# Two-layer encoder on one core: the feed-forward block in column order, with a pair's products reordered and the down lo parts on VectorE

## The chip, the cores and the metric

One of the cores of a Trainium2 chip runs the whole program. Its engines are TensorE (PE; its weight loads are listed as PEld), VectorE (DVE), ScalarE (ACT), GpSimd (POOL) and SyncE (SP), which issues nearly all transfers. The metric is the device time of one execution in microseconds, median of the runs shown.

## What is computed

```python
for l in range(DEPTH):                     # 2 layers
    x = x + hybrid_mixer(rms_norm(x, norm_mix[l]), ...)            # neighbourhood + grouped-query attention
    x = x + memory_cross_attention(rms_norm(x, norm_mem_q[l]), ...)
    x = x + conv_ffn(rms_norm(x, norm_ffn[l]), w_up[l], conv_w[l], conv_b[l], w_down[l])
return rms_norm(x, norm_final)

def conv_ffn(h, w_up, conv_w, conv_b, w_down):
    u = h @ w_up                                                    # (512, 1024) @ (1024, 5632)
    up = jnp.pad(u, ((0, 0), (1, 1), (0, 0)))
    u = up[:, :-2] * conv_w[0] + up[:, 1:-1] * conv_w[1] + up[:, 2:] * conv_w[2] + conv_b
    gate, val = jnp.split(u, 2, axis=-1)
    return (jax.nn.silu(gate) * val) @ w_down                       # (512, 2816) @ (2816, 1024)
```

There are 512 tokens on a grid of 8 rows and 64 columns, and the width is 1024. The convolution runs over the sequence, in which a token's neighbour is the next column of its row. All is float32.

## The kernel before

Activations are kept transposed: channels on the 128 partitions, the 512 tokens along a row. `xT` holds the 1024 channels in 8 chunks. The tokens stand there in column order: 8 grid rows of one column side by side, then the next column. So the sequence neighbour of a token lies 8 places on, and where a grid row ends, at the row's end of another place.

Every float32 product is made of three reduced-precision ones: an operand is split into a rounded part (`hi`, written by ACT) and the rest (`lo`, written by DVE or POOL as the difference), and `mm3` adds hi x hi, hi x lo and lo x hi in one PSUM bank.

The feed-forward block works through 22 channel pairs (a gate and a value block of 128 channels each). The first `N_PLAIN` pairs are *plain*: 24 products of 512 columns a side (`up_project`), whose sum is multiplied by the norm's factor on the way (`rep`), since the norm is not known when they start. The others are *grouped* pairs (`up`): the product of the two sides is built from seven smaller ones of 256 columns, for which DVE, ACT and POOL form sums of the weight blocks (`combined`: parts "11", "12", "22" and s1 to s4) and once a layer sums of the normed activations (`operands`: "11", "21", "22", t1 to t4). Seven products of 12 matmuls make 84 of 256 columns. A pair's last product is put off behind the first products of the next pair (`left`, `finish_up`).

`up_finish` evicts a pair: ACT multiplies by the middle tap and adds the bias, DVE adds the two neighbour taps, ACT applies SiLU to the gate, DVE multiplies gate and value, ACT and DVE write the product's hi and lo part into `acts`. Before, the block ran in row order: closing rows of the norm, scalings by `rep`, operand building and storing of activations had one side of the access pattern strided (`rows`, `lines`), so that a convolution tap was one shift by one place.

The activations of the first 16 pairs (but 2 and 3) lie in two buffers of the tag `xg`, of which there are two, and which hold the normed input until the last plain pair has read it. With them go *grouped downs* (`down_grouped`): in 16 steps of 24 products of 512 columns the activations of four pairs are multiplied and added to `xT`. `behind(n)` says which of these steps follow pair n. The remaining pairs are multiplied in `down` or `down_last`.

PSUM has 8 banks: 4 with the tag `mm`, 2 each with `sc` and `tr`. Weights come through three `raw` buffers in the order of `weights()`, and a letter there says who writes the lo part ("P" POOL, "D" DVE).

The order of the instructions is not the order of the code. All calls are taped first; then a planner runs through the tape with costs of its own for each instruction, under the plans of `PLANS` (patience, reach, a margin, rounds), and issues the whole program in the best order that it finds. An engine executes its list strictly in order.

## Time and profile before

| | before |
|---|---|
| median of 3 runs | 1319.98 us (1318.95 to 1320.20) |
| profiled execution | 1318.78 us, span 1316.9 us, clock 0.999 |
| PE busy | 1295.7 us (98%), 7557 matmuls |
| DVE busy | 1118.4 us (85%), 1805 instructions |
| ACT busy | 811.6 us (62%) |
| POOL busy | 738.6 us (56%) |
| the first layer's feed-forward block | about 292 to 660 us |
| the second layer's | about 943 to the end |

In the profile an instruction is named by what it writes and reads: `xg<-t,xg` writes an activation's lo part from a temporary `t` and its hi part in `xg`; `lo<-raw,hi` is a weight's lo part; `hi<-t,hi`, `lo<-t,lo` and `r<-raw,r` are lo parts of the weight sums and blocks of a grouped pair; `t<-sc,par,t` and `t<-tr,minus,t` are convolution taps; `mm`, `sc`, `tr` are PSUM tiles. Since every call passes through one helper, all rows have the same line, L400, and rows are told apart by their names. Matmuls overlap their successors, so a row's mean for one is longer than the distance from start to start.

### The profile page before, as it was taken

The page shows a single profiled execution, that of the slowest core. Times are in us where ns is not written, and L with a number is a line of the kernel's source. Part 1 is how long each engine was busy: PE and PEld are TensorE (multiplying, and loading weights), DVE is VectorE, ACT ScalarE, POOL GpSimd, SP SyncE. Part 2 cuts the span into 40 slices and gives each one's busy share as a digit, 9 for nine tenths or more (in the row PEclk, how much of TensorE's full clock was granted, in tenths as well). Part 3 has the DMA queues.
Part 4 walks back from the last instruction along what each step waited for, and adds up shares of the span by engine and source line. Part 5 has one row for each costly group of instructions (what it writes and reads, how often), then busy time and mean ns, then how long its engine had stood idle before and what let it go on. Part 6 is the DMA issues. An engine that isn't in the chain of part 4 may idle for free.

```text
span 1316.9 us, 20628 instructions
## 1 busy us (share of the span) xinstructions
PE 1295.7 (98%) x7557; PEld 1137.1 (86%) x7557; DVE 1118.4 (85%) x1805; ACT 811.6 (62%) x1526; POOL 738.6 (56%) x559
## 2 busy tenths in 40 slices
PE   9999999999999999999999999999999999999998
PEld 8898888887779999999888988888787899999997
DVE  8689896769999999998655898966799999999874
ACT  7777686565655656555537767765646556555552
POOL 4555867626645556544727557774456455554460
PEclk9999999999999999999999999999999999999999
DMA  8742313313222332233355422232132232233331
GB/s 279 235 129 64 97 49 98 95 49 97 80 80 97 110 115 97 97 97 112 122 159 176 129 74 72 80 97 81 48 112 64 83 111 96 98 114 113 100 106 65
DMA packets 42901, 137.48 MB, mean 104 GB/s; under 512 B 5040, under 2 KB 8496, under 8 KB 42800
## 3 DMA queue, kind: packets, MB, share of 16 engines
q1 hardware_dynamic: 42224, 135.51, 32.4%
q8 instruction: 60, 0.98, 0.3%
q10 hardware_dynamic: 576, 0.66, 0.1%
q14 instruction: 41, 0.34, 0.1%
HBM read 126.18 MB, written 2.10 MB: 97 GB/s over the span
## 4 chain that ended last, share of the span: by engine, by line
PE 77%; DVE 19%; issue 2%; ACT 1%; DMA 1%; POOL 0%; SPq 0%; DVEq 0%; ACTq 0%
PE mm L400 47%; PE sc L400 15%; PE tr L400 15%; DVE t L400 7%; DVE r L400 3%; DVE xg L400 2%; DVE lo L400 1%; DVE mm L400 1%; DVE xT L400 1%; DVE sc L400 1%; DVE hi L400 1%; DVE tr L400 1%; ACT r L400 1%; DVE s L400 0%; DMA raw<-in_w 0%
## 5 line engine op out<-in xcount | busy, mean ns | idle before, releaser
L400 POOL TENSOR_TENSOR lo<-raw,hi 128x512 fp32r<-128x512 f32 (+2 forms) x196 | 341.9, 1758 | 265.6 <-ACT hi L400 250.7
L400 PE MATMUL mm<-xg,hi 128*128 128x512 f32 (+1 forms) x898 | 282.3, 393 | 5.1 <-ACT xg L400 2.5
L400 ACT CAST hi<-raw 128x512 fp32r<-128x512 f32 (+2 forms) x212 | 160.4, 782 | 71.5 <-PE mm L400 29.3
L400 PEld LDWEIGHTS mm<-xg,hi 128*128 128x128 f32 x898 | 164.2, 188 | 39.5 <-DVE xg L400 6.6
L400 PE MATMUL mm<-r,hi 128*128 128x512 f32 (+1 forms) x608 | 193.1, 388 | 0.4 <-DVE xg L400 0.4
L400 PE MATMUL mm<-xg,lo 128*128 128x512 f32 (+1 forms) x449 | 174.9, 389 | 0.0
L400 POOL TENSOR_TENSOR t<-raw,raw 128x512 f32<-128x512 f32 x64 | 92.7, 1469 | 139.2 <-DMA raw<-in_w 117.4
L400 PE MATMUL sc<-r,r 128*128 128x256 f32 (+1 forms) x760 | 132.9, 309 | 0.0
L400 PEld LDWEIGHTS mm<-r,hi 128*128 128x128 f32 x608 | 112.2, 188 | 22.4 <-DVE xg L400 1.2
L400 PE MATMUL mm<-r,lo 128*128 128x512 f32 (+1 forms) x336 | 123.2, 367 | 0.0
L400 PE MATMUL sc<-r,hi 128*128 128x256 f32 (+1 forms) x800 | 113.2, 288 | 0.7 <-ACT t L400 0.7
L400 PEld LDWEIGHTS sc<-r,r 128*128 128x128 f32 x760 | 106.3, 191 | 5.9
L400 PE MATMUL mm<-hi,xg 128*128 128x512 f32 (+1 forms) x384 | 108.0, 357 | 0.0
L400 POOL TENSOR_SCALAR t<-t,s 128x512 f32<-128x512 f32 (+1 forms) x112 | 66.8, 612 | 73.0 <-DVE s L400 63.4
L400 PE MATMUL tr<-r,lo 128*128 128x256 f32 x768 | 102.9, 283 | 3.8 <-ACT t L400 3.8
L400 PEld LDWEIGHTS sc<-r,hi 128*128 128x128 f32 x800 | 102.7, 192 | 3.2 <-ACT t L400 2.0
L400 DVE TENSOR_TENSOR r<-raw,r 128x512 fp32r<-128x512 f32 x96 | 102.9, 1083 | 2.0 <-ACT r L400 1.8
L400 POOL TENSOR_TENSOR t<-t,raw 128x512 f32<-128x512 f32 x64 | 101.1, 1579 | 4.9
L400 PE MATMUL tr<-r,r 128*128 128x256 f32 x768 | 102.7, 283 | 0.6 <-DVE t L400 0.6
L400 PEld LDWEIGHTS tr<-r,r 128*128 128x128 f32 x768 | 98.7, 191 | 3.8 <-issue 1.4
L400 PEld LDWEIGHTS tr<-r,lo 128*128 128x128 f32 x768 | 96.7, 192 | 4.4 <-ACT t L400 4.4
L400 PEld LDWEIGHTS mm<-xg,lo 128*128 128x128 f32 x449 | 84.4, 188 | 17.3
(158 smaller groups left out, 2845.8 us busy)
## 6 DMA issues: line engine op xcount, KB each, us to landing
raw<-in_w SPq DMA_DIRECT2D x207, 512.0 KB, 3.6
r<-r SPq DMA_DIRECT2D x30, 256.0 KB, 3.5
r<-in_bias SPq DMA_DIRECT2D x16, 384.0 KB, 5.1
raw<-in_w SPq DMA_DIRECT2D x8, 384.0 KB, 3.1
r<-in_memT SPq DMA_DIRECT2D x4, 512.0 KB, 6.5
xT<-in_w SPq DMA_DIRECT2D x7, 256.5 KB, 4.3
r<-in_w SPq DMA_DIRECT2D x9, 128.0 KB, 4.1
t<-in_memT SPq DMA_DIRECT2D x4, 256.0 KB, 5.9
```

What stands on the lines that cost most here:

```text
L400: call(*args, **kwargs)
```

## The change

The feed-forward block stays in column order throughout. The closing rows, the scalings, the operand building and the stores lose their strided views; the convolution's taps shift by 8 places, in two pieces a tap: 504 columns, and 7 more where the neighbour lies in the next grid row. `N_PLAIN` goes from 6 to 7. Plain pairs are evicted in the order in which they are computed, pair j-2 after pair j, with the stores of all seven kept for the end; banks alternate by j % 4. In a grouped pair the product "12" x "21" moves from second to fifth place, while the previous pair's last product still stands behind the second. The grouped downs' steps follow other pairs (two each behind pairs 9 and 12), the activations of pairs 8 to 11 go to other places of the ring (`SLOTS`), the lo parts of their weights are written by DVE, and the planner is given six plans of four rounds in place of three of three.

```diff
-N_PLAIN = 6
+N_PLAIN = 7
...
+SLOTS = {j: j % KC if j < 8 or j > 11 else (2, 3, 0, 1)[j - 8] for j in range(N_GROUPED)}
...
 def behind(n):
-    return [] if n < N_PLAIN else range(0 if n == N_PLAIN else n - BEHIND, min(n - BEHIND + 1, N_GROUPED))
+    at = lambda r: (7, 8, 9, 9, 10, 11, 12, 12)[r] if r < 8 else r + BEHIND
+    return [r for r in range(N_GROUPED) if at(r) == n]
...
-PLANS = [((60.0, 300.0, 300.0, 300.0, 0.0), 300, margin, ASIDE, 3) for margin in (40.0, 80.0, 120.0)]
+PLANS = [((60.0, *[patience] * 3, 0.0), 300, margin, ASIDE, 4) for patience in (60.0, 120.0) for margin in (80.0, 120.0, 160.0)]
...
             hi, lo = self.ops[c]
-            if self.gcol == G_FFN:
-                hi, lo = (v.rearrange("p (r c) -> p c r", r=ROWS) for v in (hi, lo))
-                src = src.rearrange("p (c r) -> p c r", r=ROWS)
...
-                us[side] = get_w(("up", j, side)), ps_mm() if j < 2 else ps_t() if side else ps_s()
+                us[side] = get_w(("up", j, side)), ps_mm() if j % 4 < 2 else ps_t() if side else ps_s()
...
-                    DVE.tensor_mul(lines(pm), lines(pm), rows(ffn.rep))
-                up_finish(j, pms)
+                    DVE.tensor_mul(pm, pm, ffn.rep)
+                return up_finish(j, pms)
+            stores = []
             for j in range(2, N_PLAIN):
...
-                if j < 4:
-                    finish(j)
-            for j in (0, 1, *range(4, N_PLAIN)):
-                finish(j)
+                stores.append(finish(j - 2))
+            for j in range(N_PLAIN - 2, N_PLAIN):
+                stores.append(finish(j))
+            for store in stores:
+                store()
...
-                    DVE.scalar_tensor_tensor(lines(v), rows(xT[k]), par[:, l, G_FFN + k : G_FFN + k + 1], rows(ffn.psum),
+                    DVE.scalar_tensor_tensor(v, xT[k], par[:, l, G_FFN + k : G_FFN + k + 1], ffn.psum,
...
-            product(y, w["12"], "21", True)
-            finish_up()
             product(v, w["s1"], "t1", True)
             ACT.copy(p5, v)
+            finish_up()
             product(x, w["s2"], "t2", False)
             ACT.copy(sums[:, 1], x)
+            product(y, w["12"], "21", False)
             product(v, w["s4"], "22", False)
...
-                DVE.scalar_tensor_tensor(cc[:, 1:], u[:, : S - 1], w[0], cc[:, 1:], op0=ALU.mult, op1=ALU.add)
-                DVE.scalar_tensor_tensor(cc[:, : S - 1], u[:, 1:], w[2], cc[:, : S - 1], op0=ALU.mult, op1=ALU.add)
+                for wi, dst, src in (
+                    (w[0], slice(8, S), slice(0, S - 8)),
+                    (w[0], slice(1, 8), slice(S - 8, S - 1)),
+                    (w[2], slice(0, S - 8), slice(8, S)),
+                    (w[2], slice(S - 8, S - 1), slice(1, 8)),
+                ):
+                    DVE.scalar_tensor_tensor(cc[:, dst], u[:, src], wi, cc[:, dst], op0=ALU.mult, op1=ALU.add)
...
-            hi, lo = (rows(v) for v in acts[j])
-            ACT.copy(hi, lines(cs[0]))
-            DVE.tensor_sub(lo, lines(cs[0]), f(hi))
+            def store():
...
+                hi, lo = acts[j]
+                ACT.copy(hi, cs[0])
+                DVE.tensor_sub(lo, cs[0], f(hi))
+
+            return store
...
-        return placed(("down", g, m), "w_down", [*range(4 * g, 4 * g + 4)] * 2, [P * m] * 4 + [P * (m + 4)] * 4, "P")
+        return placed(("down", g, m), "w_down", [*range(4 * g, 4 * g + 4)] * 2, [P * m] * 4 + [P * (m + 4)] * 4, "D")
```

Three places show how instructions move. The first is DVE's list in the first layer's plain pairs. Before (`mm_753`, `mm_766` are the two sides of pair 0, `mm_770`, `mm_783` those of pair 1, `sc_824`, `tr_828` those of pair 3, `hi_846` a weight sum of the first grouped pair):

```order
L400 TENSOR_TENSOR mm_783<-mm_783,rep_760 128x512
L400 SCALAR_TENSOR_TENSOR t_850<-mm_753,par,t_850 128x511
L400 TENSOR_TENSOR r_834<-t_832,r_833 128x512
L400 SCALAR_TENSOR_TENSOR t_851<-mm_766,par,t_851 128x511
L400 SCALAR_TENSOR_TENSOR t_856<-sc_824,par,t_856 128x511
L400 SCALAR_TENSOR_TENSOR t_857<-tr_828,par,t_857 128x511 x2
L400 SCALAR_TENSOR_TENSOR t_856<-sc_824,par,t_856 128x511
L400 SCALAR_TENSOR_TENSOR t_854<-mm_770,par,t_854 128x511
L400 TENSOR_TENSOR hi_846<-t_843,hi_846 128x512
```

Now, right behind the norm's factor (`xT_76,par,tr_761` are the first instructions of the operand building):

```order
L404 TENSOR_TENSOR mm_753<-mm_753,rep_760 128x512
L404 TENSOR_TENSOR mm_766<-mm_766,rep_760 128x512
L404 SCALAR_TENSOR_TENSOR t_771<-xT_76,par,tr_761 128x512
L404 TENSOR_TENSOR mm_770<-mm_770,rep_760 128x512
L404 SCALAR_TENSOR_TENSOR t_772<-xT_78,par,tr_761 128x512
L404 TENSOR_TENSOR r_775<-t_771,r_775 128x256
L404 SCALAR_TENSOR_TENSOR t_792<-xT_76,par,tr_761 128x512
L404 SCALAR_TENSOR_TENSOR t_776<-t_776,t_772 128x256
L404 SCALAR_TENSOR_TENSOR t_798<-mm_753,par,t_798 128x504
L404 SCALAR_TENSOR_TENSOR t_777<-t_776,t_772 128x256
L404 SCALAR_TENSOR_TENSOR t_798<-mm_753,par,t_798 128x7
```

The convolution of pair 0 has moved from behind that of later pairs, among the weight sums of the first grouped pair, to the head of the block.

The second place is DVE's list in a step of the grouped pairs. Before:

```order
L400 TENSOR_TENSOR sc_963<-sc_963,t_965 128x512
L400 TENSOR_TENSOR lo_977<-t_974,lo_977 128x512
L400 TENSOR_TENSOR lo_979<-t_972,lo_979 128x512
L400 TENSOR_TENSOR hi_978<-t_975,hi_978 128x512
L400 SCALAR_TENSOR_TENSOR t_991<-sc_963,par,t_991 128x511 x2
L400 TENSOR_TENSOR r_971<-raw_938,r_971 128x512
L400 TENSOR_TENSOR xg_853<-t_967,xg_852 128x8x64
L400 TENSOR_TENSOR r_993<-raw_962,r_993 128x512
L400 TENSOR_TENSOR xT_76<-xT_76,mm_981 128x512
```

Now:

```order
L404 SCALAR_TENSOR_TENSOR t_1030<-sc_999,par,t_1030 128x504
L404 TENSOR_TENSOR xT_77<-xT_77,mm_1006 128x512
L404 TENSOR_TENSOR xg_867<-t_1003,xg_866 128x512
L404 TENSOR_TENSOR r_1032<-raw_1005,r_1032 128x512
L404 SCALAR_TENSOR_TENSOR t_1030<-sc_999,par,t_1030 128x7
L404 SCALAR_TENSOR_TENSOR t_1030<-sc_999,par,t_1030 128x504
L404 TENSOR_TENSOR xT_79<-xT_79,mm_1007 128x512
L404 SCALAR_TENSOR_TENSOR t_1030<-sc_999,par,t_1030 128x7
L404 TENSOR_TENSOR lo_1023<-raw_998,hi_1022 128x1024
L404 TENSOR_TENSOR r_1033<-raw_1019,r_1033 128x512
```

The two taps of a side have become four instructions in place of two, the store of an activation (`xg_867`) is contiguous, and a down weight's lo part of 1024 columns (`lo_1023`) has come in.

The third place is POOL's list in the same stretch. Before:

```order
L400 TENSOR_TENSOR lo_912<-raw_889,hi_911 128x1024
L400 TENSOR_TENSOR t_925<-raw_890,raw_908 128x512
L400 TENSOR_TENSOR t_924<-raw_890,raw_908 128x512
L400 TENSOR_TENSOR t_926<-t_924,raw_890 128x512
L400 TENSOR_TENSOR t_927<-t_926,raw_908 128x512
L400 TENSOR_TENSOR lo_936<-raw_913,hi_935 128x1024
```

Now:

```order
L404 TENSOR_TENSOR t_1036<-raw_1005,raw_1019 128x512
L404 TENSOR_TENSOR t_1035<-raw_1005,raw_1019 128x512
L404 TENSOR_TENSOR t_1037<-t_1035,raw_1005 128x512
L404 TENSOR_TENSOR t_1038<-t_1037,raw_1019 128x512
L404 TENSOR_TENSOR t_1060<-raw_1025,raw_1043 128x512
```

Only the four weight sums of a pair are left there.

More of the change, by code (lines that the diff above doesn't have):

```diff
@@ L1511, in encoder_kernel @@
         acts = {}
-        rows = lambda v: v.rearrange("p (c r) -> p r c", r=ROWS)
-        lines = lambda v: v.rearrange("p (r c) -> p r c", r=ROWS)
         def up_project(j, side, ks, us):
             if us[side] is None:
-                us[side] = get_w(("up", j, side)), ps_mm() if j < 2 else ps_t() if side else ps_s()
+                us[side] = get_w(("up", j, side)), ps_mm() if j % 4 < 2 else ps_t() if side else ps_s()
             w, pm = us[side]
@@ L1627, in last @@
                 product(x, w["22"], "t4", False)
-                up_finish(j, [gate, val], True)
+                up_finish(j, [gate, val], True)()
             left.append(last)
@@ L1650, in up_finish @@
             DVE.tensor_mul(cs[0], cs[0], cs[1])
-            if j < N_GROUPED and j not in (2, 3):
-                if not ring:
-                    ring.extend(xpool.tile([P, KC, S], F32R, tag="xg", name=nm("xg"), bufs=2) for _ in range(2))
-                acts[j] = [v[:, j % KC] for v in ring]
-            else:
-                acts[j] = rpair()
-            hi, lo = (rows(v) for v in acts[j])
-            ACT.copy(hi, lines(cs[0]))
-            DVE.tensor_sub(lo, lines(cs[0]), f(hi))
+            def store():
+                if j < N_GROUPED and j not in (2, 3):
+                    if not ring:
+                        ring.extend(xpool.tile([P, KC, S], F32R, tag="xg", name=nm("xg"), bufs=2) for _ in range(2))
+                    acts[j] = [v[:, SLOTS[j]] for v in ring]
+                else:
+                    acts[j] = rpair()
+                hi, lo = acts[j]
+                ACT.copy(hi, cs[0])
+                DVE.tensor_sub(lo, cs[0], f(hi))
+            return store
         ring = []
```

## The prediction

> **What bounds the kernel now.** I read the page first, then busy time by stage of the two feed-forward blocks, then TensorE's waits there, then the chain of waits, and last the groups of instructions.
>
> ```profile
> span 1316.9 us, 20628 instructions
> PE 1295.7 (98%) x7557; PEld 1137.1 (86%) x7557; DVE 1118.4 (85%) x1805; ACT 811.6 (62%) x1526; POOL 738.6 (56%) x559
> PE 77%; DVE 19%; issue 2%; ACT 1%; DMA 1%; POOL 0%; SPq 0%; DVEq 0%; ACTq 0%
> ```
>
> TensorE is busy for 98%; whatever the change brings has to come out of some 21 us of idle TensorE. The profiled execution took 1318.78 us, 1.88 us more than its span and 1.20 us below the median of 1319.98. I make the sum against 1318.78 and add 1.2 at the end.
>
> By stage (us, then busy us and count of PE, PEld, DVE, ACT, POOL; clock; DMA):
>
> ```profile
> 292.00:312.00 20.00, 18.48 (x77) 13.41 (x76) 19.48 (x27) 13.00 (x17) 12.26 (x9) 1.00 0.17 56
> 340.00:395.00 55.00, 50.52 (x262) 42.52 (x261) 54.62 (x70) 32.82 (x51) 29.43 (x17) 1.00 0.24 77
> 395.00:487.00 92.00, 91.35 (x633) 85.40 (x632) 91.23 (x103) 53.34 (x89) 52.10 (x31) 1.00 0.31 104
> 487.00:625.00 138.00, 138.00 (x967) 129.72 (x966) 128.10 (x150) 79.39 (x132) 73.81 (x44) 1.00 0.32 103
> 990.00:1046.00 56.00, 51.51 (x267) 43.37 (x266) 55.66 (x70) 33.80 (x53) 29.95 (x17) 1.00 0.24 76
> ```
>
> The first layer's block starts near 292. TensorE idles 1.5 us while the last norm rows close, 4.5 us from 340 to 395 (last plain pairs, first grouped pair), 0.65 us in the next six pairs and nothing after. The second layer repeats it (4.5 us from 990 to 1046). DVE is 99% busy wherever TensorE waits. The chain of waits from 290 to 395 names it, and the timeline shows the waits (start, duration, in brackets the idle time and its releaser):
>
> ```profile
> by line: DVE t L400 34.8%; DVE xg L400 12.8%; DVE r L400 11.6%; issue 8.0%; DVE mm L400 6.3%; DVE sc L400 5.4%; DVE xT L400 5.0%; DVE lo L400 4.9%; DVE tr L400 4.3%; DVE hi L400 2.5%; POOL s L400 2.2%; DVE s L400 1.3%; ACT xg L400 1.2%; ACT
> ...
> 298.74 0.39 PE L400 MATMUL mm<-r,lo 128*128 128x512 f32 x1
> 300.24 0.74 PE L400 MATMUL mm<-xg,hi 128*128 128x512 f32 x2 [1.11 <-DVE xg L400]
> 302.45 0.68 PE L400 MATMUL mm<-xg,hi 128*128 128x512 f32 x2
> 303.20 0.98 PE L400 MATMUL mm<-xg,hi 128*128 128x512 f32 x2
> ...
> 341.71 0.70 PE L400 MATMUL tr<-xg,hi 128*128 128x512 f32 x2 [1.36 <-DVE t L400]
> ...
> 375.56 1.69 PE L400 MATMUL tr<-r,lo 128*128 128x256 f32 x12 [1.53 <-ACT t L400]
> 378.49 1.20 PE L400 MATMUL mm<-xg,hi 128*128 128x512 f32 x4 [1.24 <-ACT xg L400]
> ```
>
> At 341 a plain pair waits for a PSUM bank whose predecessor DVE has not finished; at 375 and 378 the first grouped pair and the first down product wait for activations of pairs 0 and 1, which DVE evicted late. So the start of the block is DVE-bound, the rest TensorE-bound with DVE at its heels.
>
> **The change, part by part.** *TensorE's work.* One more plain pair in each layer: 48 products of 512 columns for 84 of 256. From start to start, in a stretch without waits:
>
> ```profile
> 441.66 1.60 PE L400 MATMUL sc<-r,r 128*128 128x256 f32 x12
> 443.10 1.60 PE L400 MATMUL tr<-r,r 128*128 128x256 f32 x12
> ...
> 452.37 0.61 PE L400 MATMUL mm<-xg,hi 128*128 128x512 f32 x2
> ...
> 453.05 0.61 PE L400 MATMUL mm<-xg,hi 128*128 128x512 f32 x2
> ```
>
> Twelve of 256 take 1.44 us, 0.120 each; three of 512 (two and one) take 0.68, 0.227 each. 48 x 0.227 - 84 x 0.120 = +0.82 us a layer, **+1.7 us**, certain because TensorE has no slack. Reordering a pair's products costs TensorE nothing; it starts with the sums' operands and needs the block "12" last.
>
> *Strided operands go.* DVE and ACT groups (busy us, mean ns):
>
> ```profile
> L400 DVE TENSOR_TENSOR sc<-sc,t 128x512 f32<-128x512 f32 x32 | 22.0, 688 | 1.0 <-PE sc L400 1.0
> L400 DVE SCALAR_TENSOR_TENSOR t<-xT,par,tr 128x512 f32<-128x512 f32 x16 | 18.8, 1206 | 0.0
> L400 DVE TENSOR_TENSOR tr<-tr,rep 128x512 f32<-128x512 f32 x8 | 9.1, 1133 | 0.0
> L400 DVE SCALAR_TENSOR_TENSOR r<-mm,s,r 128x512 fp32r<-128x512 f32 x8 | 5.9, 748 | 8.8 <-ACT r L400 8.8
> L400 DVE SCALAR_TENSOR_TENSOR xg<-sc,par,xg 128x512 fp32r<-128x512 f32 x4 | 4.4, 1152 | 0.0
> L400 DVE SCALAR_TENSOR_TENSOR r<-mm,s,r 128x128 fp32r<-128x128 f32 x8 | 2.8, 344 | 1.0 <-ACT r L400 1.0
> L400 DVE TENSOR_SCALAR s<-s,s 128x1 f32<-128x1 f32 x96 | 17.4, 205 | 0.4
> L400 DVE TENSOR_TENSOR lo<-raw,hi 128x1024 fp32r<-128x1024 f32 x8 | 11.4, 1451 | 0.1
> ...
> L400 ACT CAST hi<-t 128x512 fp32r<-128x512 f32 x64 | 39.6, 619 | 8.0 <-POOL t L400 7.8
> L400 ACT CAST xg<-t 128x512 fp32r<-128x512 f32 x28 | 33.3, 1205 | 23.3 <-DVE t L400 23.3
> ```
>
> Column order makes these contiguous. A scaling by the norm falls from 1.13 to 0.69, the operand building from 1.21 to 0.75, the lo part of a closing row from 1.15 to 0.75, ACT's casts from 1.2 to 0.62. Up to the first grouped pair DVE saves, in a layer, 12 x 0.44 + 8 x 0.46 + 8 x 0.40 = 12 us in a stretch whose chain is DVE; the seventh plain pair gives back about 6 us there (two scalings, four conv passes, a product and a lo part), but TensorE is given 10.9 us more in the same stretch. The convolution now shifts by 8 columns: two pieces of 504 and two of 7 a side in place of two of 511. A 7-wide piece stands nowhere in the trace. Bounds: 0.13 us (several `s<-s,s` of 0.205 run overlapped) and 0.344 (the 128-wide form); the two sizes of `r<-mm,s,r` extrapolate to 0.22. I take 0.18 with some overlap, nearest to the 1-wide row: four a pair, +0.7 us.
>
> [...]
>
> *Closing rows.* The last row's chain is ACT's hi, then DVE's lo: 0.5 + 0.4 = 0.9 us shorter, against the 1.27 us that TensorE loses from 298.74 (1.50 from start to start less 0.227). At 303.20 two products take 0.98 instead of 0.68; that throttling by rows of 1.15 us happens twice and goes too. I take 1.2 us a layer (bounds 0.5 and 2.0): **-2.4 us**.
>
> *Arrival-order eviction.* Pairs 0 and 1 are scaled, convolved and multiplied as soon as their sums stand, pairs 4 and 5 take `mm` banks so that `tr` and `sc` come round less often, and only the stores wait for the last plain pair. The waits 1.36, 1.53 and 1.24 go, each with some 0.16 of overlap around it, and 0.3 at 368: 4.9 us a layer, and I count **-9.8 us**. What is late next is the operand building, which holds one of the two `tr` banks until its last instruction.
>
> *Down lo parts on DVE.* This loads the engine that has no idle time. In the six pairs from 395 to 487:
>
> ```profile
> L400 DVE TENSOR_TENSOR r<-raw,r 128x512 fp32r<-128x512 f32 x18 | 22.9, 1273 | 0.1
> L400 DVE TENSOR_TENSOR hi<-t,hi 128x512 fp32r<-128x512 f32 x12 | 12.8, 1068 | 0.0
> L400 DVE TENSOR_TENSOR lo<-t,lo 128x512 fp32r<-128x512 f32 x12 | 11.7, 1011 | 0.0
> L400 DVE TENSOR_TENSOR xg<-t,xg 128x512 fp32r<-128x512 f32 x7 | 10.3, 1476 | 0.0
> L400 DVE TENSOR_TENSOR t<-t,t 128x512 f32<-128x512 f32 x6 | 7.9, 1322 | 0.1
> ...
> L400 POOL TENSOR_TENSOR lo<-raw,hi 128x1024 fp32r<-128x1024 f32 x7 | 18.5, 2640 | 19.3 <-ACT hi L400 17.4 <-PE mm L400 1.9
> ```
>
> Instructions with both inputs in SBUF take 1.01 to 1.32 us on average where one with a PSUM input takes 0.69: they stand still while POOL works. Surplus over 0.69 (1.13 for the strided xg): 18 x 0.58 + 12 x 0.38 + 12 x 0.32 + 7 x 0.35 + 6 x 0.63 = 25 us, against 52.1 us of POOL busy: 0.48 us of standstill for each us of POOL. So DVE's 15.2 us a pair are 11.1 of its own and 4.1 of standstill. After: 11.1 + 1.2 (a lo part of 1024 without standstill, from 0.69 and its 512 more columns; 1.45 with) - 0.45 (contiguous xg) + 0.7 = 12.5, and POOL's time falls from 8.7 to (52.1 - 18.5) / 6 = 5.6, so standstill to 2.7: **15.2 us of DVE against 15.5 of TensorE** (84 x 0.120 + 24 x 0.227). It fits, barely, and two of the first six pairs now carry two grouped products (5.5 us more for TensorE, 2.6 for DVE). I charge 1.5 us of new waits a layer (bounds 0 and 8), **+3 us**. Behind a late DVE stand the operands of the next pair, `tr` and `sc` banks, and the down lo parts themselves, three raw buffers deep.
>
> [...] Moving 2.4 us off POOL for 1.2 on DVE lowers their sum, but a lo part on DVE can now itself be held; that is the rival below.
>
> The planner draws up the whole program anew, so rows move elsewhere too; TensorE idles so little there that I allow ±1 us and count nothing.
>
> Sum: 1.7 - 2.4 - 9.8 + 3.0 = -7.5; 1318.8 - 7.5 = 1311.3 profiled, **1312.5 us** as a median.
>
> **The rivals.** *A: slower, DVE becomes the bound of the grouped pairs.* Place: DVE's queue between two pairs. If standstill stays at 4.1 us because the additional two-input instruction meets POOL as often, and the 7-wide pieces cost 0.22 in full, a step takes 12.7 + 4.1 = 16.8 us, 1.3 over. Over 14 steps that is 18 us, less 6 for the two double steps and about 4 that two banks of each kind can absorb: 8 to 10 us a layer. 1.7 - 2.4 - 9.8 + 19 = +8.5: **1328 us**. It decides from a step of about 16.3 us on. For it: DVE is at 99% today, and every us put on it is real. Against it: POOL loses a third of its time.
>
> *B: the waits only move.* The store of pairs 0 and 1 still needs the activation buffer, which opens only when the last plain pair has been multiplied; and the `tr` bank of the operand building comes free at about the same point as its next user. If half of the 9.8 us stays and 3 us of new waits come, 1.7 - 2.4 - 4.9 + 6 = 0: **1320 us**. Against it: the work between (convolution, multiplication) is done earlier, and only 0.62 + 0.69 us a pair remain behind the buffer.
>
> *C: better than forecast.* No new waits, all of the closing throttle gone and the 0.65 us in mid-block too: 1.7 - 4 - 11 = -13: **1306.5 us**.
>
> **How the numbers follow.** Forecast 0.57, C 0.13, B 0.17, A 0.13. A difference under 0.2% (2.6 us) can't be told from none. Faster: forecast and C, 0.70, with a little of B, 0.71; same: the rest of B and the weak end of the forecast, 0.16; slower: A, 0.13. The forecast's own range, from its bounds, is 1308 to 1317. The range that holds 8 in 10 takes in most of C and B and the mild part of A: 1306 to 1322.
>
> **What would show it.** Right: the stretch that answers to 340 to 395 has TensorE idle under 1.5 us in place of 4.5, the row at 298 shows under 0.5, DVE's two-input rows with a mean near 0.95, POOL busy lower by some 75 us, DVE busy near 1118 still, at 97% in the grouped pairs. Wrong: TensorE waits from the second grouped pair on, released by DVE hi, lo or r, with two-input means above 1.1 (A), or idle time near 350 and 380 as before under other names (B). A 7-wide row with a mean over 0.3 would break the sum's weakest term.

## The result, and the profile after

The changed kernel takes **1303.78 us** (median; 1303.15 to 1304.09) where the kernel before took 1319.47 beside it (1317.9 to 1320.2): a ratio of 0.9882, 95% interval 0.9865 to 0.9899. The forecast was 1312.5 in a range of 1306 to 1322. The direction was right, the gain was twice the one forecast, and the time fell below the range. The span went from 1316.9 to 1301.1 us.

The page of the changed kernel (span; busy time of each engine; the chain of waits by engine):

```profile
span 1301.1 us, 20672 instructions
PE 1291.9 (99%) x7485; PEld 1135.6 (87%) x7485; DVE 1066.1 (82%) x1999; ACT 777.3 (60%) x1510; POOL 655.8 (50%) x523
PE 94%; POOL 1%; DVE 1%; issue 1%; ACT 1%; DMA 0%; SPq 0%; DVEq 0%; POOLq 0%
```

DVE's share of the chain went from 19% to 1%, TensorE's from 77% to 94%. DVE executes 194 more instructions and is busy for 52 us less. By stage, with the columns of the prediction's table; the rows answer to the block's start, the stretch around the first grouped pair, the first and the later grouped pairs, and the first grouped pair of the second layer:

```profile
292.00:312.00 20.00, 20.00 (x91) 16.59 (x90) 18.62 (x31) 12.39 (x21) 12.66 (x9) 1.00 0.34 100
340.00:395.00 55.00, 55.00 (x290) 47.48 (x290) 55.00 (x91) 32.81 (x54) 28.79 (x18) 1.00 0.30 95
395.00:503.00 108.00, 108.00 (x731) 100.37 (x730) 103.69 (x158) 59.29 (x106) 43.48 (x28) 1.00 0.35 113
503.00:616.00 113.00, 113.00 (x789) 106.12 (x789) 93.66 (x151) 58.66 (x102) 42.08 (x27) 1.00 0.29 91
990.00:1038.00 48.00, 48.00 (x262) 41.81 (x261) 48.00 (x82) 28.82 (x49) 22.17 (x14) 1.00 0.28 88
```

TensorE does not idle in any of them, where it had idled 1.5 us at the start and 4.5 us a layer around the first grouped pair. From 340 to 395 DVE is still busy without a gap, but nothing waits for it any more. The last closing row and the first product that reads the normed input, in the timeline (start, duration):

```profile
301.02 0.39 PE L404 MATMUL mm<-r,lo 128*128 128x512 f32 x1
301.24 0.61 PE L404 MATMUL mm<-xg,hi 128*128 128x512 f32 x2
```

They follow each other in 0.22 us, where 1.50 stood before. DVE's groups (busy us, mean ns), over the whole program:

```profile
L404 DVE TENSOR_TENSOR r<-raw,r 128x512 fp32r<-128x512 f32 x90 | 81.6, 912 | 1.0 <-ACT r L404 0.9
L404 DVE TENSOR_TENSOR lo<-raw,hi 128x1024 fp32r<-128x1024 f32 x40 | 55.9, 1402 | 2.0 <-ACT hi L404 2.0
L404 DVE TENSOR_TENSOR hi<-t,hi 128x512 fp32r<-128x512 f32 x60 | 48.4, 807 | 3.9 <-ACT hi L404 3.9
L404 DVE TENSOR_TENSOR lo<-t,lo 128x512 fp32r<-128x512 f32 x60 | 44.9, 750 | 0.0
L404 DVE TENSOR_TENSOR xg<-t,xg 128x512 fp32r<-128x512 f32 x28 | 27.2, 975 | 0.2
L404 DVE SCALAR_TENSOR_TENSOR t<-sc,par,t 128x7 f32<-128x7 f32 x72 | 15.3, 213 | 0.0
L404 DVE SCALAR_TENSOR_TENSOR t<-xT,par,tr 128x512 f32<-128x512 f32 x16 | 11.7, 733 | 0.0
```

The operand building is at 0.73 us in place of 1.21. The two-input rows have come down although nothing was changed in them. In the first grouped pairs, 395 to 503 us, seven pairs long:

```profile
L404 DVE TENSOR_TENSOR r<-raw,r 128x512 fp32r<-128x512 f32 x22 | 23.7, 1079 | 0.2 <-ACT r L404 0.2
L404 DVE TENSOR_TENSOR hi<-t,hi 128x512 fp32r<-128x512 f32 x14 | 11.8, 846 | 0.0
L404 DVE TENSOR_TENSOR lo<-raw,hi 128x1024 fp32r<-128x1024 f32 x8 | 10.5, 1318 | 0.0
L404 DVE TENSOR_TENSOR lo<-t,lo 128x512 fp32r<-128x512 f32 x13 | 8.7, 678 | 0.0
L404 DVE TENSOR_TENSOR xg<-t,xg 128x512 fp32r<-128x512 f32 x8 | 8.1, 1013 | 0.1
L404 DVE TENSOR_TENSOR t<-t,t 128x512 f32<-128x512 f32 x8 | 6.9, 871 | 0.0
```

Where the 15.8 us of span came from can be summed over TensorE. I take the distance from the start of each product of 512 or 256 columns to the start of the next, less the distance that its kind has where nothing waits (0.227 us and 0.120 us, the medians of both traces). This excess is 37.7 us before and 20.2 after, 17.5 less. The stretch up to and around the first grouped pair (312 to 395 us, and the same of the second layer) gives 11.7 of it, the start of the block with the closing rows (291 to 312) 6.1, the middle pairs 1.8. The rest of the program lost 2.1: ahead of the first block the excess rose from 8.0 to 10.7. The seventh plain pair costs 1.6, so 15.8 remain. The waits that TensorE still has in the whole program, its own sequencer's left out:

```profile
PE sc L404 <- ACT t L404: 0.9, 2, 0.5
PE tr L404 <- DVE t L404: 0.7, 1, 0.7
PE tr L404 <- POOL t L404: 0.4, 1, 0.4
PE sc L404 <- ACT xg L404: 0.3, 1, 0.3
```

Of these 0.7, 0.5 and 0.3 stand ahead of 292 us, in the first layer's attention, where the kernel before had none. So within the feed-forward blocks no wait of this length is new, but outside of them some are.

### The profile page after: what moved, and what is told of

Read it like the earlier page. It is cut to its first block, busy times and chain, and to the rows that moved or that the text cites. A ratio compares the mean times of both kernels' runs of the same rounds, so it can differ in the third digit from the quotient of the medians.

```text
span 1301.1 us, 20672 instructions
## 1 busy us (share of the span) xinstructions
PE 1291.9 (99%) x7485; PEld 1135.6 (87%) x7485; DVE 1066.1 (82%) x1999; ACT 777.3 (60%) x1510; POOL 655.8 (50%) x523
## 4 chain that ended last, share of the span: by engine, by line
PE 94%; POOL 1%; DVE 1%; issue 1%; ACT 1%; DMA 0%; SPq 0%; DVEq 0%; POOLq 0%
PE mm L404 55%; PE sc L404 20%; PE tr L404 20%; POOL lo L404 1%; ACT t L404 0%; POOL s L404 0%; DVE t L404 0%; DVE r L404 0%; DVE s L404 0%; DMA xT<-in_w 0%; ACT r L404 0%; POOL t L404 0%; DVE mm L404 0%; DVE sc L404 0%; POOL r L404 0%
## 5 line engine op out<-in xcount | busy, mean ns | idle before, releaser
L404 POOL TENSOR_TENSOR lo<-raw,hi 128x512 fp32r<-128x512 f32 (+2 forms) x168 | 265.8, 1599 | 185.8 <-ACT hi L404 179.9
L404 PE MATMUL mm<-xg,hi 128*128 128x512 f32 (+1 forms) x1026 | 319.3, 391 | 0.0
L404 POOL TENSOR_TENSOR t<-raw,raw 128x512 f32<-128x512 f32 x60 | 86.5, 1463 | 290.4 <-DMA raw<-in_w 213.8
L404 PEld LDWEIGHTS mm<-xg,hi 128*128 128x128 f32 x1026 | 188.4, 188 | 35.5
L404 PE MATMUL mm<-xg,lo 128*128 128x512 f32 (+1 forms) x513 | 199.7, 389 | 0.0
L404 PEld LDWEIGHTS mm<-xg,lo 128*128 128x128 f32 x513 | 96.3, 188 | 20.2
L404 PE MATMUL sc<-r,hi 128*128 128x256 f32 (+1 forms) x752 | 106.7, 288 | 0.0
L404 PE MATMUL tr<-r,lo 128*128 128x256 f32 x720 | 96.2, 283 | 0.0
L404 PE MATMUL tr<-r,r 128*128 128x256 f32 x720 | 96.1, 283 | 0.0
L404 ACT ACTIVATE t<-sc,s,s 128x512 f32<-128x512 f32 (+1 forms) x96 | 68.1, 711 | 29.2 <-DVE s L404 25.8
```

Source lines behind the costliest of these rows:

```text
L404: call(*args, **kwargs)
```

## The experiments

Eighteen kernels were run. All ratios are to the kernel before, with their 95% intervals. The planner draws the whole program anew for each, so a difference of a microsecond or two between two kernels can come from another order as well as from the edit.

### One part of the change undone

**The lo parts back on POOL.**

```diff
-        ... [P * m] * 4 + [P * (m + 4)] * 4, "D")
+        ... [P * m] * 4 + [P * (m + 4)] * 4, "P")
```

> The changed kernel with one letter undone: the lo parts of the grouped downs' weights are written by POOL again (32 subtractions of 1024 columns). Theory L (standstill): these subtractions hold POOL for 2.5 us each and stop DVE's two-input instructions meanwhile, so DVE's step of a grouped pair goes from about 14.8 back to 15.5 us or more, TensorE waits again in the grouped pairs, 3 to 6 us in all, and the time is 1307 to 1310 us; POOL busy rises by about 75 us, DVE busy does not fall although 39 us of its own work leave it. Rival O (the order and the contiguous operands did it all): no TensorE wait returns, 1303 to 1305 us.

1305.61 us, 0.9892 [0.9878, 0.9907]: at most 2 us worse than the change. POOL's work rises to 732.6 us and TensorE's only wait from 292 to 500 us is

```profile
PE sc L404 <- ACT t L404: 0.8, 1, 0.8
```

DVE's busy time is 1075.2 us, 9 more than in the changed kernel, although 39 us of its work have gone to POOL: it stands still for longer. `r<-raw,r` goes from 912 to 1117 ns on average, `hi<-t,hi` from 807 to 951. So the standstill that the expectation's theory L speaks of does return, but TensorE hardly feels it: undone alone, the move to DVE is worth 2 us at most.

**The old product order, and the old plans** (two kernels; each puts the lines of before back).

> The changed kernel with the old order of products in a grouped pair (block 12 second again). Theory P (the block's parts are written last and were waited for): the waits of 0.8 us in mid-block return and some 1 to 2 us a layer at the first grouped pair, 1306 to 1309 us. Rival: DVE is ahead by now, so it makes no difference, 1303 to 1305 us.

> The changed kernel with the three old plans of the planner. If the additional plans carry part of the gain: waits of 1 to 4 us appear anywhere in the program, 1305 to 1308 us. If they don't: 1303 to 1305 us, which also says how far a newly drawn order alone moves the time.

1305.05 us, 0.9892 [0.9877, 0.9907], and 1302.47 us, 0.9872 [0.9854, 0.9889]. Neither can be told from the changed kernel.

**Six plain pairs.** First with the table of grouped-down steps left as it is, then with the table moved forward by a pair.

```diff
-N_PLAIN = 7
+N_PLAIN = 6
 ...
-    at = lambda r: (7, 8, 9, 9, 10, 11, 12, 12)[r] if r < 8 else r + BEHIND
+    at = lambda r: (6, 7, 8, 8, 9, 10, 11, 12)[r] if r < 8 else r + BEHIND   # second kernel only
```

> The changed kernel with six plain pairs instead of seven; the table of the grouped downs stays. TensorE has 1.7 us less to do. Theory C (the seventh plain pair is cover: 10.9 us of TensorE's work in front of the first grouped pair for some 6 us of DVE's, at a place where DVE is busy for 55.00 of 55 us): waits of 2 to 5 us a layer return near the first grouped pair, 1306 to 1312 us. Rival N (eviction in order of arrival alone gives DVE enough room): no wait returns, 1301.5 to 1302.5 us, faster than the changed kernel.

> The changed kernel with six plain pairs and its table of grouped-down steps moved forward by a pair where the step has its activations, so that the first step stands behind pair 6 as it did before. In the earlier run with six plain pairs the table stayed. If that loss of 14 us came from the missing cover alone, it stays: 1314 to 1322, with waits of 1 to 3 us near 370 and 396. If it came from the table's steps standing one pair too late for six plain pairs, most of it goes: 1303 to 1309.

With the old table 1317.58 us, 0.9985 [0.9975, 0.9994]: nearly all of the gain gone, and more lost than either expectation had. TensorE's waits from 292 to 400 us, and the windows around the last of them:

```profile
PE tr L404 <- DVE t L404: 1.9, 1, 1.9
PE sc L404 <- ACT hi L404: 1.4, 1, 1.4
PE sc L404 <- DVE hi L404: 1.2, 1, 1.2
```

```profile
397.00:399.00 2.00, 0.18 (x1) 0.21 (x2) 2.00 (x6) 1.04 (x1) 0.00 (x0) 1.00 0.04 14
399.00:401.00 2.00, 2.00 (x12) 2.00 (x12) 2.00 (x5) 0.00 (x0) 0.00 (x0) 0.57 0.00 0
```

I first read this as proof that the seventh pair is the cover under which DVE catches up. The second kernel refutes that: 1303.19 us, 0.9875 [0.986, 0.989], the same as seven pairs. What cost 14 us was the table: with the old one no grouped-down step stands behind the first grouped pair, so that two grouped pairs follow each other with nothing in between for TensorE to do while DVE forms their operands. With a table that fits, the seventh plain pair is worth nothing that can be measured.

**Late eviction** of the pairs 0, 1 and 4 to 6, with the old banks and with the new ones.

```diff
-                stores.append(finish(j - 2))
+                if j < 4:
+                    finish(j)()
 ...
+            for j in (0, 1, *range(4, N_PLAIN)):
+                finish(j)()
 ...
-    ps_mm() if j % 4 < 2 else ...
+    ps_mm() if j < 2 else ...          # first kernel only
```

> The changed kernel with the eviction of plain pairs 0, 1, 4, 5 and 6 at the end of the plain pairs again and with the former banks; all else stays. Theory O (order): the three waits near the first grouped pair return, 5 us a layer, 1312 to 1315 us. Theory S (DVE's time): DVE has gained 12 us a layer by contiguous operands, so at most 1 us a layer returns, 1304 to 1306 us.

> Late eviction of pairs 0, 1, 4, 5 and 6 as before, but with the new rotation of banks. The kernel with late eviction and the old banks lost 22 us, most of it in one wait of 5.5 us a layer for a bank. If the banks did that: 1308 to 1314 us, with waits only at the first down product. If the lateness itself did it: 1320 us or more, with the wait at a bank of another tag.

1326.2 us, 1.0048 [1.0033, 1.0063], slower than either theory had it, and 1342.1 us, 1.0178 [1.0163, 1.0193]. TensorE's largest wait in the first layer, with the old banks:

```profile
PE sc L404 <- DVE t L404: 5.4, 1, 5.4
```

and with the new ones:

```profile
PE mm L404 <- DVE t L404: 14.4, 1, 14.4
```

A plain pair waits for a bank whose predecessor DVE has not convolved. With the new rotation pair 4 takes an `mm` bank that pair 0 or 1 held, and as long as such a bank is emptied late the wait is the longer for it. So the arrival order is needed for all of the gain: without it the rest of the change is slower than the kernel before. That is not to say that it brings the gain by itself; see the kernels with one part alone.

**Row order**, with the strided views and the taps of 511 put back, and then the same with a planner that knows what strides cost.

```diff
+                    DVE.tensor_mul(lines(pm), lines(pm), rows(ffn.rep))   # and the other views of before
 ...
+            busy += 0.88 * n * strided     # second kernel only: the planner's cost, DVE, ns a column
+            busy += 1.14 * n * strided     # ACT
```

> The changed kernel in row order again (strided closing rows, scalings, operand building and stores, taps as shifts by one place in one piece); eviction in order of arrival, seven plain pairs, the new order of products and DVE's lo parts stay. Theory S (the strides cost DVE its time ahead of the first grouped pair): the closing rows' waits return, 2.1 us a layer, and DVE is 12 us a layer later, so waits of 2 to 5 us a layer return near the first grouped pair: 1312 to 1318 us. Rival O (order of eviction alone removed the waits at the start): only the closing rows' waits return, 1307 to 1309 us.

> The changed kernel in row order (1334 us) with one thing more: the planner's costs know of the strides (0.88 ns a column more on DVE, 1.14 on ACT, from the rows 1.13 against 0.69 and 1.20 against 0.62). Theory W (the plan was wrong: it took strided instructions for contiguous ones, so the order it drew up could not be kept): half or more of the 30 us comes back, 1312 to 1320 us. Theory S (DVE has not the time, whatever the order): 1328 to 1336 us.

1334.39 us, 1.0102 [1.0083, 1.0121], much worse than expected; with true costs 1315.74 us, 0.9974 [0.9963, 0.9984]. So of the 30 us that row order loses, 19 go with another plan, and 12 are left in the better of the two plans. I read the 19 as the price of a plan drawn with the times of contiguous operands, but this is not shown, since the same costs do not help the kernel before:

> The kernel before with the same true costs of strides in the planner and nothing else changed. Theory W: the waits near the first grouped pair shrink by half, 1312 to 1316 us, a part of the gain that needs no change of the arithmetic. Theory S: 1318 to 1322 us.

1335.1 us, 1.0118 [1.0103, 1.0134], slower by 16; neither expectation holds. A wait of 7.3 us stands ahead of the first down product. With the late eviction order the truer costs led to a worse order, so a newly drawn order can by itself move the time by nearly as much as the 19 us above.

### One part alone, in the kernel before

**The seventh plain pair** (`N_PLAIN = 7`).

> The kernel before with seven plain pairs in place of six, and nothing else; its grouped downs move back by one pair with it. Theory C (the seventh plain pair is cover for VectorE ahead of the first grouped pair and pays by itself): part of the 4.5 us a layer that TensorE waits at the first grouped pair goes, 1312 to 1317. Theory K (cover pays only where the plain pairs are evicted in order of arrival; with late eviction the seventh pair is one more pair that VectorE has to catch up with): no gain, 1319 to 1328, with the waits of before at the first grouped pair as long or longer.

1338.55 us, 1.014 [1.0121, 1.0159], above even theory K's range. The pair waits for `tr` banks (timeline; in brackets the idle time and its releaser):

```profile
342.77 0.47 PE L400 MATMUL tr<-xg,hi 128*128 128x512 f32 x1 [2.90 <-DVE t L400]
...
378.64 1.19 PE L400 MATMUL tr<-xg,hi 128*128 128x512 f32 x2 [6.79 <-DVE t L400]
```

With late eviction one more plain pair is one more that DVE has to catch up with.

**The lo parts on DVE** ("P" to "D").

> The kernel before with nothing changed but the letter: DVE writes the lo parts of the grouped downs' weights. Theory L: POOL holds DVE less, so the two waits of 0.8 us in mid-block go and DVE reaches the first down product no later: 1317 to 1319 us. Rival A of the prediction (DVE becomes the bound): DVE's step goes over 15.5 us and TensorE waits in the grouped pairs, 1322 to 1330 us.

1333.34 us, 1.0103 [1.0086, 1.0119], above rival A's range, but not by its mechanism. The stage around the first grouped pair, and its two largest waits:

```profile
340.00:395.00 55.00, 46.30 (x224) 39.17 (x224) 53.73 (x65) 29.72 (x44) 22.17 (x14) 0.94 0.22 68
```

```profile
PE mm L400 <- ACT xg L400: 4.9, 1, 4.9
PE tr L400 <- DVE t L400: 3.8, 2, 2.9
```

TensorE idles 8.7 us there, against 4.5 before. From 395 to 495 it is busy for 99.36 of 100 us. The edit hurts only where DVE is late with evictions; the grouped pairs bear it.

**Column order alone** (the views and the taps).

> The kernel before, in column order and with nothing else changed (six plain pairs, late eviction, POOL's lo parts, the old order of products, the old plans). Theory S: the closing waits (4.2 us in both layers) and most of the waits near the first grouped pair go (up to 10 us), while the grouped pairs get 0.4 us of DVE each: 1306 to 1311 us. Theory O: only the closing waits go, 1314 to 1317 us.

1314.12 us, 0.9964 [0.9951, 0.9978], where theory O had it. The closing rows' waits are gone; a wait for activations is left in each layer's block, of 2.1 us in the first and in the second of

```profile
PE mm L400 <- ACT xg L400: 7.6, 1, 7.6
```

**Column order and arrival order together**, then with the new table, and its places of the ring, as well.

```diff
-                if j < 4:
-                    finish(j)
+                stores.append(finish(j - 2))       # b_column's edits, banks by j % 4, stores at the end
 ...
+    at = lambda r: (6, 7, 8, 8, 9, 10, 11, 12)[r] if r < 8 else r + BEHIND   # second kernel only
```

> The kernel before in column order and with eviction in order of arrival (banks by j % 4, stores at the end), and nothing else of the change: six plain pairs, the old table of grouped-down steps (two steps behind pair 6), the old product order, POOL's lo parts, the old plans. Theory P (these two parts carry the gain): 1303 to 1307, TensorE's waits at the first grouped pair under 1 us a layer. Theory Q (the gain needs what surrounds them too, the table of steps above all, since the table that was wrong by a pair cost 14 us): 1308 to 1318, with waits of 1 to 3 us near 370 and 1015 left over.

> The kernel before in column order, with eviction in order of arrival, and the new table of grouped-down steps moved forward by a pair for six plain pairs (one step behind pair 6 in place of two, two behind pair 8; places of the ring with it). Old product order, POOL's lo parts, old plans. Theory Q (the table is the third part and the rest carries at most 2 us each): the wait of 2.9 us for activations at the second step goes, 1302 to 1307. If the table does nothing here, 1308 to 1311 with that wait in place.

1309.57 us, 0.9934 [0.9917, 0.9951]: some 9 of the 15.7 us. The old table puts two steps behind pair 6, and in the second of them TensorE waits for an activation:

```profile
373.12 0.79 PE L400 MATMUL mm<-xg,hi 128*128 128x512 f32 x1 [2.88 <-DVE xg L400]
```

With the new table 1314.86 us, 0.9963 [0.9947, 0.9979]: not better, slower than either expectation, and the wait stands in the first step:

```profile
374.86 1.19 PE L401 MATMUL mm<-xg,hi 128*128 128x512 f32 x2 [2.92 <-DVE t L401]
```

This kernel differs from the fast one with six plain pairs only in the product order, the lo parts' engine and the plans, and loses 11.7 us by them, though each of the three, undone alone in the changed kernel, costs 2 us at most. From 340 to 372 us this kernel

```profile
340.00:372.00 32.00, 31.94 (x158) 26.98 (x157) 31.41 (x44) 16.54 (x27) 21.97 (x15) 1.00 0.24 79
```

stands against the fast kernel with six plain pairs:

```profile
340.00:372.00 32.00, 32.00 (x158) 27.14 (x157) 32.00 (x51) 18.48 (x32) 17.02 (x12) 1.00 0.20 65
```

The same 158 matmuls, but DVE got through 51 instructions beside 17.0 us of POOL in place of 44 beside 22.0. In the fast kernel the lo parts of the activations of two pairs are written just in time (timeline of both engines):

```profile
367.92 1.28 DVE L404 TENSOR_TENSOR xg<-t,xg 128x512 fp32r<-128x512 f32 x2
...
369.79 0.63 PE L404 MATMUL mm<-xg,hi 128*128 128x512 f32 x2
```

0.6 us before their use, against 2.9 us too late. So here it is a question of a few microseconds of DVE ahead of the first down product, and several parts can each bring them. Which of the three does it, or whether it is the order that the planner happens to find, was not separated.

### How much room DVE has

**Each grouped down's lo part written two and three times by DVE**, which leaves the result as it is.

```diff
+            for _ in range(1 if key[0] == "down" and len(key) == 3 else 0):     # 2 in the second kernel
+                DVE.tensor_sub(lo[:, k], raw[:, k], f(hi)[:, k])
```

> The changed kernel with each lo part of the grouped downs' weights written twice by DVE (the second write repeats the first): 16 more instructions of about 1.3 us a layer, DVE's step from 14.8 to some 16.1 us against TensorE's 15.5. The prediction's rival A put the point from which DVE decides at 16.3 us and charged 1.5 us of waits a layer at 15.2. If DVE's room is as narrow as that: waits of 3 to 8 us a layer, 1310 to 1320 us, most of them from the second grouped pair on. If the room is larger than I thought (DVE idles for 4 us in the first seven pairs and for 19 us in the next seven): under 2 us a layer, 1304 to 1308 us.

> The changed kernel in which VectorE writes each grouped down's lo part three times (the second and third writing leave the result as it is): 32 instructions of 1.0 to 1.4 us more a layer, in a step of about 14.7 + 2 x 1.15 us of own work and standstill against 15.5 of TensorE. If VectorE has a bound near 16.3 us a step, it is passed: waits between grouped pairs from the second step on and 1318 or more. If the work that is put on VectorE only moves other work of it to ScalarE's and GpSimd's side of the order, as the doubling looked (4.4 us in all), it stays under 1314.

Twice: 1308.2 us, 0.992 [0.9903, 0.9936]. Thrice: 1341.2 us, 1.0165 [1.014, 1.0189]. The first and the later grouped pairs, written twice:

```profile
395.00:503.00 108.00, 107.30 (x721) 99.34 (x720) 107.65 (x162) 56.97 (x100) 37.48 (x24) 1.00 0.32 103
503.00:616.00 113.00, 113.00 (x792) 106.25 (x791) 106.30 (x168) 59.95 (x108) 44.78 (x30) 1.00 0.32 103
```

and three times, with the largest of TensorE's waits from 385 to 640:

```profile
395.00:503.00 108.00, 100.55 (x662) 92.49 (x663) 105.74 (x157) 51.29 (x91) 36.00 (x23) 0.98 0.28 88
503.00:616.00 113.00, 108.85 (x748) 100.50 (x747) 111.77 (x168) 57.08 (x102) 41.62 (x26) 1.00 0.30 94
```

```profile
PE mm L404 <- DVE lo L404: 5.4, 3, 2.7
```

The step of the first stretch, seven pairs, is 107.65 / 7 = 15.4 us when they are written twice. In the changed kernel DVE idles 108 - 103.69 = 4.3 us in the first of these stretches and 113 - 93.66 = 19.3 in the second, 23.7 us a layer. A second writing adds 16 parts of about 1.21 us (the mean of `lo<-raw,hi` in the first stretch, written twice), 19.4 us, which fits; a third makes it 38.8, which does not: 15 us a layer too much, 30 in two layers, and 37 were measured (the granted clock also fell, to 0.98 in the first stretch). In the second stretch DVE went from 93.66 to 106.30 to 111.77 us of 113. The room is one of the whole run of grouped pairs, not of one step.

**Without the 7-wide pieces.** This kernel leaves out the neighbours across the end of a grid row.

```diff
-                    (w[0], slice(1, 8), slice(S - 8, S - 1)),
-                    (w[2], slice(S - 8, S - 1), slice(1, 8)),
```

> The changed kernel without the four 7-wide pieces of a convolution (it leaves out the neighbours across the end of a grid row, so that part of the result is not computed): 176 instructions of VectorE fewer, 72 of them at 0.213 us in the largest group, 37 us of busy in all. If VectorE's time counts in the grouped pairs, some 2 to 6 us faster than the changed kernel: 1298 to 1302. If VectorE has room there, within 1.5 us of it: 1302.3 to 1305.3.

1303.79 us, 0.9877 [0.9862, 0.9892]: no difference to the changed kernel. DVE's busy time falls by 9 us only, where the pieces' own rows make up some 37. Part of the difference is standstill: `hi<-t,hi` goes from 807 to 942 ns. Part is overlap: such pieces, back to back, start 0.13 to 0.14 us apart (at 364.23, 364.37 and 364.50 us in the fast kernel with six plain pairs) where a row of them shows 0.21.

## Why the prediction was right and wrong

**Right: the place.** The forecast located the loss at two points, the closing rows and the start of the block up to the first grouped pair, and said that DVE is the bound there and TensorE elsewhere. Of TensorE's excess 17.8 us went at these two points and 1.8 in the middle pairs; 2.1 came in elsewhere.

**Near in size, not shown in cause: the arrival order**, -9.8 forecast and -11.7 measured at the place; TensorE's own work is +1.6 as forecast (twice 0.82 is 1.6; the sum had 1.7). That the gain needs the arrival order is shown by putting the late eviction back (+22 us, in a kernel with seven plain pairs). That it brings the 11.7 by itself is not shown, and it does not look so: added to column order alone it brought 1314.12 - 1309.57 = 4.6 us. The term held the work of several parts, and that its size came out is in part luck.

**The step that failed: "It fits, barely ... I charge 1.5 us of new waits a layer".** No wait of the grouped pairs came, so 3.0 us of the sum were charged for nothing. Half of the working was good: own work of 12.5 us a pair was forecast. Measured, the two-input rows of 395 to 503 have a surplus over 0.69 us (1.21 for 1024 columns) of 22 x 0.39 + 14 x 0.16 + 8 x 0.32 + 8 x 0.18 + 8 x 0.11 = 15.7 us, 2.2 a pair, so that 103.69 / 7 = 14.8 leaves 12.6 of own work. But the standstill was forecast at 2.7, because I held its share of POOL's time fixed at 0.48; it fell to 15.7 / 43.5 = 0.36. The step is 14.8 us and not 15.2. For a step of its size the charge was about right: with the lo parts written twice the step is 15.4 us, and the kernel loses 2.2 us a layer. So it is the standstill that was mis-sized, and with it the step. Rival A had a second fault: it multiplied an excess over one step by 14, less some 10 us, while the prediction's own table showed that DVE idles 10 us from 487 to 625. The two runs with more lo parts show that such slack is used: some 19 us more a layer cost only 2.2. Rival A's waits come mildly with that load, and in full with twice that load (37 us).

That DVE's two-input rows stand still while POOL works shows in both traces (timelines of DVE and POOL). Of the 96 `r<-raw,r` of 512 columns in the kernel before, the 49 with no POOL instruction beside them take 0.67 to 0.71 us, the other 47 take 0.67 to 2.37, 1.50 on average; in the changed kernel 50 take 0.68 on average and 40 take 1.20. `t<-sc,par,t` of 511 columns, with a PSUM input, takes 0.74 on average without POOL and 0.75 with it in the kernel before. The lower means and the longer busy time with the lo parts on POOL agree with it. How much of POOL's time turns into standstill is not fixed: 0.48 before and 0.36 in the changed kernel. With only the lo parts put back on POOL the same sum from 395 to 503 us is 20 x 0.42 + 12 x 0.52 + 8 x 0.88 + 12 x 0.25 + 8 x 0.46 = 28.4 us beside 65.9 of POOL, 0.43. So the share changes with what POOL does, and the move itself lowered it.

**The other step that failed, by size: the closing rows**, -2.4 forecast, -6.1 measured, the largest miss of the sum. I took 0.9 of the 1.27 us of the last row and two held-up products behind it. All of the 1.27 went, and with it 0.35 us at an earlier row (292.8 us) and three delays of 0.37, 0.37 and 0.33 us from 303 to 306, with smaller ones 3.1 us a layer. Even the upper bound of 2.0 a layer was too low.

**Not counted: the waits of the middle pairs (1.8) and what a new plan does elsewhere (2.1 the other way).** The 0.65 us in mid-block were seen, and given to rival C alone. They do not come back with the old order of products (TensorE's only wait from 292 to 500 us is of 0.3), so the new order is not what removed them. I take it that they went because DVE is no longer behind when it comes there, which no run shows. Elsewhere the prediction allowed 1 us and counted nothing. The first layer's attention became 2.7 us longer, in part by its new waits, and all places outside those named 2.1 us in sum; no run says which part of the change drew the order so.

Summed: 3.0 from the new waits, 3.7 from the closing rows, 1.9 from the stretch at the first grouped pair and 1.8 from the middle pairs, less the 2.1 elsewhere, make the 8.3 us between -7.5 and the -15.8 of the span. What came is rival C, which had 0.13; its mechanism, no new waits in the blocks and the closing and mid-block waits gone, holds, and even its -13 was too small.

**The other signs.** POOL -83 us (forecast -75). The stretch that answers to 340 to 395 has no idle time (under 1.5). DVE at 103.69 of 108 in the first grouped pairs (97% forecast, 96% measured), and the mean of its two-input rows there near the 0.95 forecast (59.2 us in 65 instructions, 0.91). DVE's total was to stay near 1118 and fell to 1066.1: the two-input rows lost more standstill than was foreseen, `hi<-t,hi` from 1179 to 807 ns and `r<-raw,r` from 1083 to 912. The 7-wide pieces take 0.213 us, not 0.18, and start 0.13 to 0.14 us apart where two follow each other directly (16 times in the changed kernel). But taking the pieces away moved nothing, so the sum's weakest term was also its least important.

**The seventh pair.** The prediction counted its 10.9 us of TensorE time as help for DVE. Alone it makes the kernel before 19 us slower, and with a table that fits the changed kernel does as well without it.

## What to carry to other kernels

Where an engine is the bound only in one stretch, read its room over the whole run of work that can absorb a delay, and not from the mean of its fullest step; then add load on purpose to see where it breaks. The order in which results are taken out of their banks can be worth more than the time of taking them out: under late eviction the seventh pair cost 19 us and the lo parts on DVE 13, and of the parts tried alone only column order still gained, 5 us. And undo more than one part at a time: three parts that cost at most 2 us each when undone alone were worth 12 together in a kernel with six plain pairs (the newly drawn order included), and a loss that looked like a missing pair was a table that no longer fitted.

## What the runs showed of the hardware that was not expected

A wait of TensorE can cost more than its length. In row order a wait of 5 us is followed by matmuls of half the speed (timeline; then windows with the granted clock as third last number):

```profile
356.93 1.22 PE L404 MATMUL tr<-xg,hi 128*128 128x512 f32 x2 [5.01 <-DVE t L404]
...
358.38 1.06 PE L404 MATMUL tr<-xg,hi 128*128 128x512 f32 x2
359.23 0.63 PE L404 MATMUL tr<-xg,lo 128*128 128x512 f32 x1
```

```profile
356.00:360.00 4.00, 3.07 (x7) 2.51 (x8) 4.00 (x4) 3.16 (x5) 4.00 (x4) 0.50 0.07 7
360.00:364.00 4.00, 4.00 (x14) 3.15 (x13) 3.17 (x5) 0.63 (x1) 1.13 (x1) 0.69 0.34 124
364.00:368.00 4.00, 4.00 (x19) 3.33 (x18) 2.72 (x3) 2.59 (x4) 1.81 (x1) 1.00 0.00 0
```

Two products of 512 columns take 359.23 - 358.38 = 0.85 us, 0.425 each in place of 0.227, and the full speed is back after some 5 us (two products from 363.02 us take 0.47). The clock also fell after a wait of 1.91 us (0.57 from 399 to 401 us, with six plain pairs and the unshifted table), and in the same kernel behind two waits of 1.42 and 1.19 us that lie 0.5 us apart (0.50 from 376 to 378 us). It did not fall after the waits of up to 1.53 us of the kernel before, nor after one of 2.94 us in the kernel before with the lo parts on DVE (1.00 from 344 to 348 us). So a wait's length alone does not decide it. How long the half rate lasts can be summed from the windows, as twice the time that the clock falls short of 1.00: 3.4 us with late eviction and the old banks (0.57 from 371 to 375 us) and in the kernel with arrival order, the new table and six plain pairs (0.70, 0.50 and 0.94 in the three windows of 2 us from 374), some 6.9 in row order (0.95 from 352 to 356, then the first two of the windows above). So the forecast's price, which equals a wait's length, holds for the waits of before; where the clock falls, half of the stretch in which TensorE works is to be added: at most 1.7 us for one of 3.4, some 2.7 here. The mean granted clock of the profiled execution is 0.987 to 0.998 in twelve of the eighteen variants and 0.999 to 1.000 in the other six; the changed kernel's is 0.999, and 1.00 from 5 to 1297 us.

The second surprise is how little the times of the variants add up. Each kernel is planned as a whole, and what decides is whether a few activations and banks are ready some microseconds before or after TensorE comes to them.
